# Softmax over rows of 1024: the first tile's load split into two 64-partition transfers on two queues, and one store moved from ACT's queue to Pool's

## The chip, the cores and the metric

The kernel runs on one core of a Trainium2 chip. The metric is the device time of one execution in microseconds (us); lower is better. Before the change the median of three runs is 317.25 us. The engines that matter here are VectorE (DVE), ScalarE (ACT) and GpSimd (Pool), and SyncE (SP), which only issues transfers. The 16 DMA engines of the core move all data between HBM, where the tensors live, and SBUF, the on-chip memory of 128 partitions in which the engines compute.

## The reference

`x` is 32 x 512 x 1024 float32, so 16384 rows of 1024 numbers, 67.11 MB; the output has the same size. The temperature is 0.5.

```python
scaled = x / temperature
shifted = scaled - np.max(scaled, axis=-1, keepdims=True)
exp_x = np.exp(shifted)
return (exp_x / np.sum(exp_x, axis=-1, keepdims=True)).astype(np.float32)
```

Each row is its own softmax. Every number is read once and written once, so 134.2 MB have to pass the DMA engines.

## The kernel before, in words

The rows are cut into 11 blocks, which the kernel calls passes. A pass is one tile `xt` of 128 partitions; passes 0 to 9 hold 12 rows in each partition (12 x 4 KB = 49152 B of consecutive memory, 6 MB in all), and pass 10 holds 8 rows (32768 B in each partition, 4 MB). Four tile buffers exist (`BUFS = 4`). A pass is worked on in place in two or three groups of 4 or 6 rows per partition (`PASSES`): pass 0 is 4, 4, 4; passes 1 to 9 are 6, 6; pass 10 is 4, 4.

For a group there are three steps. `maximum` (L69, L72) is one DVE reduction over the group's rows and one small DVE multiplication that makes the bias. `exponential` (L78) is one ACT activation per row, which also sums the row. `divide` (L90, then L93 or L96) is a small DVE reciprocal and either one DVE multiplication of the whole group (passes in `WHOLE`) or one per row.

Each engine runs its instructions in the order in which the program lists them, and the program writes that order out by hand: first four loads, then for each group g its maximum and exponential, and after them the divide of group g-1 and, when that was the last group of a pass, the store of that pass. In passes 9 and 10 the divide and the store come ahead of the next maximum (`ALONE`).

`load` (L60) issues one transfer for a whole pass from SP's queue; the profile calls that queue q1. The first four loads wait for nothing. Load 4 and the later ones are issued from inside `store`, one with each pass, and SP waits there until the store of the pass that last used the buffer has landed. `store` (L108) issues one transfer for a whole pass: from Pool's queue (q0, whose descriptors are made by software) for passes 0 to 5, which is what `BY_POOL = 6` says, and from ACT's queue (q10) for passes 6 to 10. On ACT the store stands behind the exponentials of the following group, on Pool behind nothing but the stores before it. Ahead of store 0 Pool makes a tiny copy out of tile 2 (L106), so that store 0 isn't issued before tile 2 has landed.

In the trace the first DVE reduction and ACT's load of its exponential table both start when tile 0 has landed, at 18.25 and 18.30 us.

Of the kernel before, what the change touches and what calls it, by code (L numbers as in the profile page):

```python
# [1 line left out]

# [4 lines left out]

PASSES = [[4, 4, 4]] + [[6, 6]] * 9 + [[4, 4]]  # L10
BUFS = 4

WHOLE = (2, 3, 4, 6, 8)


BY_POOL = 6

ALONE = 9


@with_exitstack
def kernel(
    ctx: ExitStack,
    tc: tile.TileContext,
    x: bass.AP,
    temperature: bass.AP,
    out: bass.AP,
):
    nc = tc.nc
    f32 = mybir.dt.float32  # L30
    scale = 1.0 / float(temperature)
    extreme = mybir.AluOpType.max if scale > 0 else mybir.AluOpType.min

    P = 128
    xf = x.flatten_outer_dims()
    of = out.flatten_outer_dims()
    n, d = xf.shape
    rows = [sum(ks) for ks in PASSES]
    assert sum(rows) * P == n

    data = ctx.enter_context(tc.tile_pool(name="data", bufs=BUFS))
    stats = ctx.enter_context(tc.tile_pool(name="stats", bufs=4))


    groups = []
    for i, ks in enumerate(PASSES):
        for j, k in enumerate(ks):
            groups.append((i, sum(ks[:j]), k))

    def dram(t, i):  # L50
        block = t[P * sum(rows[:i]) : P * sum(rows[: i + 1]), :]
        return block.rearrange("(p k) d -> p k d", p=P, k=rows[i])

    tiles, small = [], []

    def load():
        i = len(tiles)
        if i < len(PASSES):
            xt = data.tile([P, rows[i], d], f32, name="xt")
            nc.sync.dma_start(out=xt, in_=dram(xf, i))  # L60
            tiles.append(xt)

    def maximum(g):
        i, a, k = groups[g]
        top, bias, sums, recip = (
            stats.tile([P, k], f32, name=name) for name in ("top", "bias", "sums", "recip")
        )
        small.append((bias, sums, recip))
        nc.vector.tensor_reduce(  # L69
            out=top, in_=tiles[i][:, a : a + k, :], axis=mybir.AxisListType.X, op=extreme  # L70
        )
        nc.vector.tensor_scalar_mul(bias, in0=top, scalar1=-scale)  # L72

    def exponential(g):
        i, a, k = groups[g]
        bias, sums, _ = small[g]
        for b in range(k):
            nc.scalar.activation(  # L78
                tiles[i][:, a + b, :],
                tiles[i][:, a + b, :],  # L80
                mybir.ActivationFunctionType.Exp,
                bias=bias[:, b : b + 1],
                scale=scale,
                accum_out=sums[:, b : b + 1],
            )

    def divide(g):
        i, a, k = groups[g]
        _, sums, recip = small[g]
        nc.vector.reciprocal(recip, sums)  # L90
        if i in WHOLE:
            xt = tiles[i][:, a : a + k, :]
            nc.vector.tensor_mul(xt, xt, recip.unsqueeze(2).to_broadcast([P, k, d]))  # L93
            return
        for b in range(k):
            nc.vector.tensor_scalar_mul(  # L96
                tiles[i][:, a + b, :], in0=tiles[i][:, a + b, :], scalar1=recip[:, b : b + 1]
            )

    def store(g):  # L100
        i, a, k = groups[g]
        if a + k == rows[i]:
            if i == 0:


                nc.gpsimd.tensor_copy(stats.tile([P, 1], f32, name="seen"), tiles[2][:, 0, 0:1])  # L106
            queue = nc.gpsimd if i < BY_POOL else nc.scalar
            queue.dma_start(out=dram(of, i), in_=tiles[i])  # L108
            load()

    with tc.manual_schedule():
        for _ in range(BUFS):
            load()
        for g in range(len(groups) + 1):

            alone = g < len(groups) and groups[g][0] >= ALONE and groups[g][1] == 0
            if g > 0 and alone:
                divide(g - 1)  # L120
                store(g - 1)
            if g < len(groups):
                maximum(g)
                exponential(g)
            if g > 0 and not alone:
                divide(g - 1)
                store(g - 1)


# [1 line left out]
_INS = ['x', 'temperature']  # L131
_OUTS = [((32, 512, 1024), 'float32')]

_NUMBERS = {'temperature': 0.5}


# [26 lines left out]
```

## Time and profile before

| what | us |
|---|---|
| median of three runs (lowest, highest) | 317.25 (317.19, 320.41) |
| span of the profiled execution, first to last instruction | 315.8 |
| DVE busy in that span | 256.9 |
| ACT busy | 148.3 |
| Pool busy | 3.7 |
| first tile: issued, landed for DVE | 0.74, 18.25 |
| first store issued on Pool | 47.89 |
| store of pass 6 issued on ACT | 211.22 |
| last store issued on ACT | 301.35 |

The profile is of one execution and gives its span, with no other time of its own; the median of the runs lies 1.45 us above that span. A row of the page with 40 digits or numbers cuts the span into 40 slices of 7.9 us; a digit is the busy share of a slice in tenths, and 9 is 90% or more. The DMA row is the mean over the 16 DMA engines, and GB/s is what they moved, booked at the packets' starts. A DMA packet in these records is one partition's row of a tile, 49152 B or 32768 B, moved by one of the 16 engines, or one of 4 B with which an engine reports that its part of a transfer is done. In a table of windows the columns are the window, its length, the busy time of DVE, ACT and Pool with the number of instructions, the clock of TensorE (not used here), the DMA share and GB/s. In a timeline a line gives start, duration, engine, source line and operation; in brackets is the idle time ahead of it and what ended it.

### The profile page before, as it was taken

How to read it: one execution, taken by the hardware profiler on the slowest of the kernel's cores; microseconds unless marked ns; L12 is line 12 of the kernel's file. 1: busy time of each engine (PE TensorE's matmuls, PEld its weight loads, DVE VectorE, ACT ScalarE, POOL GpSimd, SP SyncE). 2: the span in 40 equal slices, each digit the busy share in tenths (PEclk: the TensorE clock that was granted, in tenths of full speed). 3: DMA queues.
4: the chain of work that ended last, by engine and by line, in shares of the span. 5: the costliest groups of instructions: out<-in, count | busy, mean ns of one | idle time of the engine just before them, and what ended most of it. 6: DMA issues, size and time to landing. Idle time of an engine off the chain costs nothing.

```text
span 315.8 us, 525 instructions
## 1 busy us (share of the span) xinstructions
DVE 256.9 (81%) x147; ACT 148.3 (47%) x257; POOL 3.7 (1%) x11
## 2 busy tenths in 40 slices
DVE  0069999999999899979976994999199999969710
ACT  0029636775461807344471744074416802953700
POOL 0000001000000000000000000000000000000000
DMA  8999999999999999999999999999999999999996
GB/s 305 473 417 423 461 411 399 399 468 430 400 479 417 417 461 411 430 467 405 442 448 399 455 442 405 467 424 417 461 417 430 455 401 463 411 452 411 455 411 270
DMA packets 3171, 134.24 MB, mean 425 GB/s; under 512 B 352, under 2 KB 352, under 8 KB 352
## 3 DMA queue, kind: packets, MB, share of 16 engines
q1 hardware_dynamic: 1584, 67.11, 49.7%
q0 software_dynamic: 864, 37.75, 27.6%
q10 hardware_dynamic: 720, 29.36, 21.5%
q14 instruction: 3, 0.02, 0.0%
HBM read 67.11 MB, written 67.11 MB: 425 GB/s over the span
## 4 chain that ended last, share of the span: by engine, by line
DMA 47%; DVE 28%; ACT 11%; issue 9%; DVEq 0%; SPq 0%; POOLq 0%
DMA xt<-in_x_dram 25%; DMA out_dram<-xt 22%; DVE top L69 16%; ACT xt L78 11%; DVE xt L96 8%; DVE xt L93 2%; DVE bias L72 0%; DVE recip L90 0%; DVEq L158 0%; SPq L60 0%; POOLq L108 0%
## 5 line engine op out<-in xcount | busy, mean ns | idle before, releaser
L78 ACT ACTIVATE xt<-xt,bias 128x1024 f32<-128x1024 f32 x128 | 145.2, 1135 | 131.7 <-DVE recip L90 70.6
L69 DVE TENSOR_REDUCE top<-xt 128x6 f32<-128x6144 f32 (+1 forms) x23 | 139.9, 6083 | 37.8 <-DMA xt<-in_x_dram 37.8
L93 DVE TENSOR_TENSOR xt<-xt,recip 128x6144 f32<-128x6144 f32 x10 | 65.6, 6558 | 0.4
L96 DVE TENSOR_SCALAR xt<-xt,recip 128x1024 f32<-128x1024 f32 x68 | 46.2, 749 | 0.5
L78 ACT ACTIVATION_READ_ACCUMULATOR xt<-xt,bias 128x1 f32 x128 | 23.9, 187 | 0.0
L78 ACT ACT_TABLE_LOAD x1 | 1.3, 1283 | 18.3 <-DMA xt<-in_x_dram 18.3
L90 DVE RECIPROCAL recip<-sums 128x6 f32<-128x6 f32 (+1 forms) x23 | 4.2, 182 | 5.0 <-ACT xt L78 5.0
L108 POOL DMA_DIRECT2D out_dram<-xt x6 | 3.3, 554 | 129.6 <-ACT xt L78 82.7
L72 DVE TENSOR_SCALAR bias<-top 128x6 f32<-128x6 f32 (+1 forms) x23 | 3.9, 171 | 0.8
L106 POOL COPY seen<-xt 128x1 f32<-128x1 f32 x1 | 0.2, 185 | 46.9 <-DMA xt<-in_x_dram 46.9
L144 POOL MEMSET const-uint8-127<- 128x1 uint8 x1 | 0.1, 103 | 0.0
L144 POOL MEMSET const-bfloat16-1.0<- 128x1 bf16 x1 | 0.1, 102 | 0.0
L144 POOL MEMSET const-float32-0.0<- 128x1 f32 x1 | 0.1, 99 | 0.2 <-issue 0.2
L144 POOL MEMSET const-float32-1.0<- 128x1 f32 x1 | 0.1, 98 | 0.0
## 6 DMA issues: line engine op xcount, KB each, us to landing
xt<-in_x_dram SPq DMA_DIRECT2D x10, 6144.0 KB, 36.4
out_dram<-xt POOLq DMA_DIRECT2D x6, 6144.0 KB, 35.9
out_dram<-xt ACTq DMA_DIRECT2D x4, 6144.0 KB, 31.9
xt<-in_x_dram SPq DMA_DIRECT2D x1, 4096.0 KB, 34.9
out_dram<-xt ACTq DMA_DIRECT2D x1, 4096.0 KB, 13.5
```

Of the source, the lines that this page charges most:

```text
L69: nc.vector.tensor_reduce(out=top, in_=tiles[i][:, a : a + k, :], axis=mybir.AxisListType.X, op=extreme)
L72: nc.vector.tensor_scalar_mul(bias, in0=top, scalar1=-scale)
L78: nc.scalar.activation(tiles[i][:, a + b, :], tiles[i][:, a + b, :], mybir.ActivationFunctionType.Exp, bias=bias[:, b : b + 1], scale=scal ...
L90: nc.vector.reciprocal(recip, sums)
L93: nc.vector.tensor_mul(xt, xt, recip.unsqueeze(2).to_broadcast([P, k, d]))
L96: nc.vector.tensor_scalar_mul(tiles[i][:, a + b, :], in0=tiles[i][:, a + b, :], scalar1=recip[:, b : b + 1])
L106: nc.gpsimd.tensor_copy(stats.tile([P, 1], f32, name="seen"), tiles[2][:, 0, 0:1])
L108: queue.dma_start(out=dram(of, i), in_=tiles[i])
L144: nc = _bacc.Bacc("TRN2", target_bir_lowering=False, num_devices=1)
```

## The change

The load of pass 0 is issued as two transfers of 64 partitions each: partitions 0 to 63 from SP's queue and partitions 64 to 127 from ACT's queue. Neither waits for anything. All other loads stay as they were. `BY_POOL` goes from 6 to 7, so the store of pass 6 is issued by Pool and no longer by ACT: Pool issues seven stores, ACT four.

```diff
-BY_POOL = 6
+BY_POOL = 7
...
             xt = data.tile([P, rows[i], d], f32, name="xt")
-            nc.sync.dma_start(out=xt, in_=dram(xf, i))
+            if i == 0:
+
+                half = P // 2
+                nc.sync.dma_start(out=xt[:half], in_=dram(xf, i)[:half])
+                nc.scalar.dma_start(out=xt[half:], in_=dram(xf, i)[half:])
+            else:
+                nc.sync.dma_start(out=xt, in_=dram(xf, i))
             tiles.append(xt)
```

## The prediction

> **What bounds the kernel now.** I read the page's slices first, then the queues, then a table of windows, then the DMA view of a few very short windows.
>
> ```profile
> DVE  0069999999999899979976994999199999969710
> ACT  0029636775461807344471744074416802953700
> DMA  8999999999999999999999999999999999999996
> q1 hardware_dynamic: 1584, 67.11, 49.7%
> q0 software_dynamic: 864, 37.75, 27.6%
> q10 hardware_dynamic: 720, 29.36, 21.5%
> ```
>
> The DMA row is full from the second slice to the last but one, while DVE, the busiest engine, starts in the third slice and has gaps to the end. The queues' shares add up to 98.8% of 16 engines' span. The queue sizes also tell how a load is cut: q1 has 1584 packets for 11 loads, 144 each, which is 128 rows and 16 reports: each of the 16 engines moves 8 partitions' rows and one report.
>
> ```profile
> 0.00:4.00 4.00, 0.00 (x0) 0.00 (x0) 0.21 (x4) 1.00 0.66 197
> 18.25:47.90 29.65, 29.23 (x24) 18.37 (x30) 0.19 (x2) 1.00 1.00 431
> 47.90:56.00 8.10, 8.03 (x6) 5.42 (x11) 0.66 (x1) 1.00 0.96 364
> 56.00:205.00 149.00, 135.16 (x63) 74.56 (x131) 2.66 (x5) 1.00 1.00 435
> 280.00:312.00 32.00, 19.08 (x21) 9.44 (x18) 0.00 (x0) 1.00 0.99 429
> ```
>
> Loads alone (18 to 48), loads with stores (56 to 205) and stores alone (280 to 312) all run at 429 to 435 GB/s and a DMA share of 0.99 or 1.00. So the end is set by the number of bytes at one fixed pace. Two places are short of it: the first microseconds, and 48 to 56, when Pool's first store joins.
>
> Next, four very short windows of the DMA view, each shorter than one packet: 1.7 to 2.5, 210 to 211, 211.85 to 212.95 and 217.3 to 218.5 us. The columns are packets, MB, share of 16 engines.
>
> ```profile
> q1 hardware_dynamic: 16, 0.79, 328.2%
> ...
> q0 software_dynamic: 15, 0.74, 171.2%
> ...
> q1 hardware_dynamic: 15, 0.74, 154.7%
> ...
> q10 hardware_dynamic: 15, 0.74, 141.9%
> ```
>
> A packet is booked where it starts, so a share gives its length: 1.547 x 16 x 1.1 us / 15 = 1.815 us for 49152 B, or 27.08 GB/s for an engine and 433 GB/s for 16. The others give 1.83 and 1.82 us on q0 and q10; the first 16 packets of the run lasted longer, 3.282 x 16 x 0.8 / 16 = 2.63 us. And the reader is to see that the engines take turns between queues in step: within 1 us, 15 of 16 start a packet of q0 and none one of q1, and a packet later it is the other way round.
>
> An engine has ten tiles x 8 rows x 2 directions = 160 packets of 1.815 us and 16 of 1.213 us (32768 B at that pace): 309.8 us. Add 1.76 us until the first packet starts, 0.81 us by which the first is longer (2.63 - 1.815), about 1.0 us in 48 to 56 ((433 - 364) x 8.1 / 433 = 1.3, part of it an artefact of booking at starts), and 1.3 us from the last packet's end at 314.5 to 315.8: 314.7 to 315.0 of 315.8 us. The median of the runs is 1.45 us above the span. I add costs to the span and carry that 1.45 along.
>
> **The change part by part.** *Store 6 from ACT to Pool.*
>
> ```profile
> 204.58 6.56 DVE L93 TENSOR_TENSOR xt<-xt,recip 128x6144 f32<-128x6144 f32 x1
> 211.22 0.97 ACTq L108 DMA_DIRECT2D out_dram<-xt  x1
> ```
>
> The divide of pass 6 ends at 211.14. ACT issues at 211.22, and the transfer's first packet starts at 217.33, since q0 still moves store 5 (its last row ends at 217.22). Pool waits for that same divide, its issue costs 0.53 us (median of its six), and its slowest start on an empty queue, store 0, is 4.4 us (47.89 to 52.26): ready at 215.5, before q0 is free. So q0 goes on at about 217.3 as q10 did. ACT loses a 0.97 us issue that lay before a wait of 6.4 us for the next bias at 217.84: nothing. If the cover were gone, store 6 would miss one turn, 1.8 us, while loads fill the engines, and load 10, which SP holds for store 6 until 246.68, would be that much later in a full queue. Pool has nothing behind store 6. I take 0, between 0 and 0.5.
>
> *The issue of the halves.* SP still issues four transfers by 2.8 us. ACT gets one more, 0.97 us as its first one cost, with 18.3 us of idle time around it:
>
> ```profile
> 0.74 2.05 SPq L60 DMA_DIRECT2D xt<-in_x_dram  x4
> 18.25 4.42 DVE L69 TENSOR_REDUCE top<-xt 128x4 f32<-128x4096 f32 x1 [18.25 <-DMA xt<-in_x_dram]
> 18.30 1.28 ACT L78 ACT_TABLE_LOAD   x1 [18.30 <-DMA xt<-in_x_dram]
> 22.91 1.15 ACT L78 ACTIVATE xt<-xt,bias 128x1024 f32<-128x1024 f32 x1 [3.33 <-DVE bias L72]
> ```
>
> Behind ACT's issue stand the table load and the first exponential, which waits for DVE until 22.91: cost 0. DVE's first maximum now needs two reports; a wait released by one shows 0.02 us of issue in the chain, so 0.02 more.
>
> *The halves themselves.* This decides. No transfer of 64 partitions is in this trace. The lower end: the limit of 27.08 GB/s belongs to each DMA engine, and all 16 share each half, four rows apiece. Then each still moves 8 packets of tile 0, and the tile lands as before; the longer first packet may hide behind the other queue's (-0.8 us), or be paid twice, or the second queue's joining costs what 48 to 56 cost (+1.0). The upper end: the limit belongs to the part of SBUF that an engine reaches. In a 128-partition transfer each engine has eight partitions of its own. In a half, 16 engines have 64 partitions between them, so two must share what one had, and since they take turns in step they are on the same half together. Each packet then lasts up to 2 x 1.815 = 3.63 us, eight in a row 29.0 instead of 14.5: +14.5 us, with no work to fill it, since the half that isn't being written waits in every engine's other queue.
>
> Which one? The pace is the same for reading HBM, writing it and both, and on three queues, so neither HBM nor the queue sets it; engine and SBUF side remain, and the trace doesn't separate them. A third arrangement is that a half goes to only eight engines: the same eight for both halves give 16 packets in a row for them, again +14.5 us, because each engine's total sets the end. A fourth, eight engines of its own for each half, is priced among the rivals. Of the four one costs nothing, and it needs both that all 16 engines serve each half and that the limit is the engine's own. I take the shared limit. The engines aren't quite in step: the 15 starts from 210 to 211 spread over 0.9 us, so two sharers overlap a little less than fully. With 0.2 us apart, each packet costs 1.815 - 0.2 = 1.6 us more, 8 x 1.6 = 13 us.
>
> [...]
>
> *What follows a late tile.* DVE starts 13 us later. From 18.25 to store 0 at 47.89 DVE is the chain (29.2 of 29.65 us busy), so store 0 goes to about 61; the loads of tiles 1 to 3 are 13 us later too, so the engines stay full and the rest of the run is moved as it stands. Sum: 315.8 + 13 + 0.02 + 0 = 328.8 span, 317.25 + 13 = 330 time.
>
> **The rivals.** *It makes no difference* (not slower). Place: the first 18 us; it decides if a 49152 B packet of a half still takes 1.815 us. For it speaks that this figure never moves between queues and directions. Tile 0 then lands near 18, at most some 4 us later if ACT's queue joins two turns late, and nothing follows from that, as loads alone keep the engines full until 2.6 + 32 x 1.815 = 60.7 us, and store 0's first packet moves only from 52.3 to 56. Time 317.25 - 0.8 to + 1.0: 316.4 to 318.3.
>
> *Each half goes to its own eight engines.* Then half two meets tile 1's rows in its engines and alternates: 16 packets, landing near 2.6 + 29 = 31.6 instead of 17.9. No engine time is wasted at first, but DVE starts 13.7 us later and store 0's first packet comes at 66, after the loads ran dry at 60.7: 5 us of idle DMA, and perhaps 2 to 4 more until store 1 follows. +5 to +9, 322 to 326. For it: nothing in the trace; against: a full transfer puts 8 rows on each engine evenly.
>
> *Faster by over 1%.* All that isn't bytes at the pace is 1.76 + 0.81 + 1.3 at the start and the join, 3.9 us, and the 1.76 stays; 3.2 us can't come out of the rest.
>
> **How the numbers follow.** Shared limit, or the same eight engines: 0.50, 326 to 332, point 330. Own eight engines: 0.08, 322 to 326. No difference: 0.40, 316.4 to 318.3. Faster by over 1%: 0.02. A measurement of this kernel can tell about 1%, 3.2 us. Slower is 0.50 + 0.08 = 0.58, same 0.40. Since neither main case may be left out, the range is 316.3 to 332; the likeliest case alone is 326 to 332.
>
> **What would show it.** Right: DVE's first reduction starts at 29 to 32 us, the DMA view of the first 18 us shows q1 and q10 packets of over 3 us and about half of 433 GB/s, and all later marks (store 0, last store) are 11 to 14 us later. Wrong: first reduction near 18 and packets of 1.8 us. Eight engines show as eight packets of a queue starting together instead of 16. Store 6 on q0 should start near the end of store 5 with no gap in the DMA share; a gap there would price the second part of the change.

## The result, and the profile after

The changed kernel takes 331.68 us (median of 6 runs, 331.43 to 332.03), the one before 317.22 beside it. The ratio is 1.0448 with a 95% interval of 1.0418 to 1.0477: 13.3 to 15.1 us slower. The profiled execution took 331.43 us and its span is 329.7, 13.9 us more than the 315.8 of before.

The page's slices and queues first, as for the kernel before. A slice is now 8.2 us.

```profile
DVE  0000799999999999999995899499589998969710
DMA  8997999999999999999999999999999999999996
GB/s 191 203 268 197 406 453 423 435 447 412 460 401 459 400 471 400 459 406 453 435 423 453 412 459 400 465 406 454 417 441 435 429 453 404 461 425 423 441 427 278
q1 hardware_dynamic: 1520, 63.96, 47.3%
q0 software_dynamic: 1008, 44.04, 30.9%
q10 hardware_dynamic: 656, 26.21, 20.7%
```

The DMA row alone would mislead: it is full from the start. The GB/s row shows what happened: four slices at 191 to 268, and from the fifth on the old pace. The engines are busy with packets that take twice as long (3.65 us against 1.815, worked out below). The table of windows says the same with DVE's part in it.

```profile
4.00:18.25 14.25, 0.00 (x0) 0.00 (x0) 0.00 (x0) 1.00 1.04 221
18.25:31.00 12.75, 0.00 (x0) 0.00 (x0) 0.00 (x0) 1.00 0.87 185
31.00:62.00 31.00, 26.41 (x20) 15.54 (x26) 0.00 (x0) 1.00 1.02 431
70.00:219.00 149.00, 138.32 (x68) 76.46 (x133) 2.66 (x5) 1.00 1.00 434
```

Until 31 us the engines are 87 to 104% busy at 185 to 221 GB/s; after that at 431 to 434 as before. Two windows of the DMA view, 9.1 to 10.5 and 12.7 to 14.1 us, show what kind of packets these are (packets, MB, share of 16 engines):

```profile
q10 hardware_dynamic: 16, 0.79, 260.4%
...
q1 hardware_dynamic: 16, 0.79, 260.7%
```

All 16 engines start a packet of the ACT half within 1.4 us, and a turn later all 16 one of the SP half. A packet lasts 2.604 x 16 x 1.4 / 16 = 3.65 us; before it was 1.815. The timeline shows the issues and the first work on the tile, Pool's stores of pass 0 and of pass 6, and ACT's last store:

```profile
0.74 0.54 SPq L63 DMA_DIRECT2D xt<-in_x_dram  x1
0.75 0.56 ACTq L64 DMA_DIRECT2D xt<-in_x_dram  x1
...
35.18 4.42 DVE L75 TENSOR_REDUCE top<-xt 128x4 f32<-128x4096 f32 x1 [35.18 <-DMA xt<-in_x_dram]
...
64.68 0.67 POOL L114 DMA_DIRECT2D out_dram<-xt  x1 [1.59 <-DVE xt L102]
225.31 0.53 POOL L114 DMA_DIRECT2D out_dram<-xt  x1 [31.19 <-issue]
314.79 0.34 ACTq L114 DMA_DIRECT2D out_dram<-xt  x1
```

The two halves are issued within 0.01 us of each other; DVE starts 16.9 us later than before.

### The profile page after: what moved, and what is told of

Its sections match the earlier page's. It is cut to its first block, busy times and chain, and to the rows that moved or that the text cites. A ratio compares the mean times of both kernels' runs of the same rounds, so it can differ in the third digit from the quotient of the medians.

```text
span 329.7 us, 532 instructions
## 1 busy us (share of the span) xinstructions
DVE 256.9 (78%) x147; ACT 148.3 (45%) x257; POOL 4.7 (1%) x12
## 4 chain that ended last, share of the span: by engine, by line
DMA 67%; DVE 19%; ACT 8%; issue 0%; DVEq 0%; SPq 0%
DMA xt<-in_x_dram 34%; DMA out_dram<-xt 33%; DVE top L75 12%; ACT xt L84 8%; DVE xt L102 7%; DVE bias L78 0%; DVE recip L96 0%; DVEq L164 0%; SPq L66 0%
```

## The experiments

Theory T: within a half of 64 partitions two DMA engines share what one has for itself in a transfer of 128, and since the engines take turns in step (16 packets to a turn, above), both are on the same half at the same time. Rivals: the second queue at the start costs the time; any transfer of fewer partitions is slow; the moved store has a part. Each ratio is to the kernel before, run on the same chip in the same series. It is worked out from the single runs and not from the medians: the kernel before had medians of 317.40 to 317.75 us in these series, and its runs in a series lay 2.4 to 3.7 us apart. Each profile is of one run. Diffs are against the kernel before; behind the first one, the test for tile 0 and the plain load are mostly left out.

**The two parts of the change, each alone.**

```diff
-            nc.sync.dma_start(out=xt, in_=dram(xf, i))
+            if i == 0:
+                nc.sync.dma_start(out=xt[:64], in_=dram(xf, i)[:64])
+                nc.scalar.dma_start(out=xt[64:], in_=dram(xf, i)[64:])
+            else:
+                nc.sync.dma_start(out=xt, in_=dram(xf, i))
```

> The load of tile 0 split into two halves of 64 partitions on SP's and ACT's queues; store 6 stays on ACT. Theory (two engines share one part of SBUF's side within a half, so a packet lasts twice 1.815 us): the whole loss is here, 331 to 332 us, the first 16 packets on q10 again at 3.6 us. Rival (moving store 6 to Pool has a part in the loss): below 330.

Measured: 333.77 us, ratio 1.0475 (1.0409 to 1.0541); the first 16 packets on q10 last 3.64 us on average. That is 1.8 us above the time expected, but not in the load: by the packet records the engines lose 17.7 us of the first 40, as in the changed kernel (17.8). They lose 3.7 us behind 290 us, where the changed kernel loses 2.1; why isn't known.

```diff
-BY_POOL = 6
+BY_POOL = 7
```

> Only the store of pass 6 is moved from ACT to Pool. Theory: no cost, 317.2 within 0.5 us. Rival (a part of the loss comes from the store): above 318.5 us, with a gap in the DMA share near 215 us.

Measured: 317.92 us, 0.2 above what was expected in a series in which the kernel before took 317.72; ratio 0.9985 (0.9956 to 1.0014), so between 1.4 us faster and 0.4 slower. The split alone loses as much as the whole change (the intervals of 1.0475 and 1.0448 overlap); the store costs nothing that can be told.

**Is it the second queue, or the half?** Both halves on one queue, and, the other way round, two queues with all partitions each.

```diff
+                nc.sync.dma_start(out=xt[:64], in_=dram(xf, i)[:64])
+                nc.sync.dma_start(out=xt[64:], in_=dram(xf, i)[64:])
```

> Both 64-partition halves of tile 0 are issued from SP's queue, one after the other; ACT issues no load. Theory (the half's partitions are what limits): every packet of tile 0 still lasts 3.6 us, eight in a row, 331 to 332 us; DVE starts earlier than the 35.2 us of the changed kernel, at 31 to 32, since no other queue's packets stand between the halves and their reports, and the total doesn't follow that start. Rival (two hardware queues fighting at the start cost the time): packets of 1.8 us and 317 to 318 us.

```diff
+                nc.sync.dma_start(out=xt[:, :6, :], in_=dram(xf, i)[:, :6, :])
+                nc.scalar.dma_start(out=xt[:, 6:, :], in_=dram(xf, i)[:, 6:, :])
```

> Tile 0 is loaded by two transfers of all 128 partitions at the same moment, rows 0 to 5 of each partition from SP's queue and rows 6 to 11 from ACT's. Theory: each engine again has eight partitions of its own, a packet of 24576 B lasts 0.91 us and the total is that of before, 316.5 to 318.5 us. Rival (two queues at the start cost the time): 331 us, packets of 1.8 us for 24576 B.

Both halves on SP: 332.88 us, 0.9 above what was expected, ratio 1.0463 (1.0402 to 1.0524). Its table of windows:

```profile
4.00:18.25 14.25, 0.00 (x0) 0.00 (x0) 0.00 (x0) 1.00 1.07 221
18.25:31.00 12.75, 0.00 (x0) 0.00 (x0) 0.00 (x0) 1.00 0.90 185
```

The same 221 and 185 GB/s with a single queue. The start at 31 to 32 was missed: the last row ends at 33.18, and DVE starts at 34.21, 1.0 us after that.

Halves by rows on two queues: 318.73 us, 0.2 above what was expected, ratio 1.0011 (0.9978 to 1.0044). Its DMA view from 6 to 8 us:

```profile
q1 hardware_dynamic: 19, 0.47, 54.3%
q10 hardware_dynamic: 16, 0.39, 45.6%
```

0.543 x 32 / 19 = 0.91 us for 24576 B on each queue (32 is 16 engines x 2 us), the full 27 GB/s. Two queues at the same moment cost nothing that can be told, at most 1.4 us; half of the partitions does (1.0463 on a single queue).

**Which partitions share?** Tile 0 in three transfers, partitions 32 to 95 from SP and the outer ones from ACT; then the same three on SP alone; then quarters.

```diff
+                nc.sync.dma_start(out=xt[32:96], in_=dram(xf, i)[32:96])
+                nc.scalar.dma_start(out=xt[:32], in_=dram(xf, i)[:32])
+                nc.scalar.dma_start(out=xt[96:], in_=dram(xf, i)[96:])
```

> Tile 0 is loaded by three transfers: partitions 32 to 95 from SP's queue, 0 to 31 and then 96 to 127 from ACT's. Theory (what two engines share is the place in SBUF of partitions 32 apart in the same half of 64): partitions 32 to 95 have no two such, so SP's packets last 1.8 us, while ACT's stay at 3.6 us; 4 x 1.8 + 4 x 3.6 = 21.8 us for the tile instead of 14.5, 324 to 325.5 us in all. Rival (any transfer over fewer than 128 partitions is slow, whichever they are): all packets 3.6 us, 331 to 334 us. [...]

Measured: 327.36 us, ratio 1.03 (1.0253 to 1.0347), 2 us more than expected. The first 16 of SP's packets last 2.45 us on average, ACT's first 16 3.64. A reading of the 2.45 us that no window shows: in this order the turns mix, and while some engines write rows of 32 to 95, others are still on an outer part. So it was run once more on one queue (the diff is against this kernel):

```diff
-                nc.scalar.dma_start(out=xt[:32], in_=dram(xf, i)[:32])
-                nc.scalar.dma_start(out=xt[96:], in_=dram(xf, i)[96:])
+                nc.sync.dma_start(out=xt[:32], in_=dram(xf, i)[:32])
+                nc.sync.dma_start(out=xt[96:], in_=dram(xf, i)[96:])
```

> As with the three transfers of partitions 32 to 95, 0 to 31 and 96 to 127 before, but all on SP's queue, in this order, so that no turn between queues mixes them. Theory (partitions 32 apart in one half of 64 share): the first four packets of each engine last 1.815 us but for the longer first one, the next four 3.6 us; tile 0 takes 21.8 us of packets instead of 14.5, +7.3 us, 324.5 to 326 us. Rival (any transfer over fewer than 128 partitions is slow): eight packets of 3.6 us, 332 us and more.

Measured: 325.61 us, ratio 1.0239 (1.0164 to 1.0314), as T priced it. The table of windows of this kernel:

```profile
4.00:10.00 6.00, 0.00 (x0) 0.00 (x0) 0.00 (x0) 1.00 0.95 401
10.00:17.00 7.00, 0.00 (x0) 0.00 (x0) 0.00 (x0) 1.00 1.05 225
17.00:24.00 7.00, 0.00 (x0) 0.00 (x0) 0.00 (x0) 1.00 1.03 218
```

And its DMA view from 6.5 to 7.9 us, in the first of these windows:

```profile
q1 hardware_dynamic: 14, 0.69, 113.5%
```

Of partitions 32 to 95 a packet takes 1.135 x 16 x 1.4 / 14 = 1.82 us, the steady pace (the 401 GB/s count packets where they start, in a short window), and directly behind them 32 partitions go twice at about 220 (225 and 218). So it isn't the number of partitions: 0 to 63 is slow (3.57 us a packet at the start of the changed kernel, 1.641 x 16 x 1.9 / 13 = 3.84 with both halves on SP, from 5.5 to 7.4 us) and 32 to 95 is not, though both read as many bytes of HBM in the same strides. That partitions 32 apart in one half share was assumed before the run, and the paces agree with it for whole blocks of 32: 0 to 31 go at 225 GB/s by themselves and, with both halves on SP, at 221 together with 32 to 63, while 32 to 63 and 64 to 95 together run at the steady pace. Which partitions of two blocks share no run here shows.

```diff
+                nc.sync.dma_start(out=xt[:32], in_=dram(xf, i)[:32])
+                nc.sync.dma_start(out=xt[32:64], in_=dram(xf, i)[32:64])
+                nc.sync.dma_start(out=xt[64:96], in_=dram(xf, i)[64:96])
+                nc.sync.dma_start(out=xt[96:], in_=dram(xf, i)[96:])
```

> Tile 0 goes as four transfers of 32 partitions from SP's queue. Theory (two engines share): packets of 3.6 us as with halves, since 32 partitions reach as many places as 64 do, 331 to 334 us. Rival (the pace falls with the number of partitions): packets of about 7.3 us and 29 us more than the halves, near 361 us.

Measured: 333.32 us, ratio 1.0487 (1.0433 to 1.0542); the first 16 packets of the four transfers average 3.67 to 3.83 us. A quarter is no slower than a half (3.65 in the changed kernel). That 32 partitions reach as many places as 64 do was assumed; the equal packets agree with it.

**Elsewhere in the run: a load in the middle, and a store.**

```diff
+            if i == 6:
+                nc.sync.dma_start(out=xt[:64], in_=dram(xf, i)[:64])
+                nc.sync.dma_start(out=xt[64:], in_=dram(xf, i)[64:])
```

> The load of tile 6, in the middle of the run, goes as two 64-partition halves from SP's queue, with stores on Pool's queue beside it. Theory: the engines keep in step between queues, so each of its packets lasts 3.6 us and the store's packets between them 1.8 us; +13 to +14.5 us, 330 to 333 us. Rival (it is a matter of the first microseconds, or stores in between take the pressure off): below 322 us.

Measured: 331.43 us, ratio 1.0402 (1.0346 to 1.0457). The DMA view from 144 to 158 us:

```profile
q1 hardware_dynamic: 51, 2.36, 65.8%
q0 software_dynamic: 41, 2.02, 35.7%
```

Of the 51 packets on q1 three are reports; 0.658 x 16 x 14 / 48 = 3.07 us for a row of the half, 1.95 for a row of the store between. A little below 3.65, and the loss near its full size (1.0402 against 1.0448): it isn't a matter of the first microseconds.

```diff
+            if i == len(PASSES) - 1:
+                nc.sync.dma_start(out=dram(of, i)[:64], in_=tiles[i][:64])
+                nc.scalar.dma_start(out=dram(of, i)[64:], in_=tiles[i][64:])
+            else:
+                queue.dma_start(out=dram(of, i), in_=tiles[i])
```

> Loads as in the kernel before; the store of the last tile is split into two halves of 64 partitions, on SP's and ACT's queues. Theory, if reading SBUF is limited as writing is: the last store's packets of 32768 B last 2.43 us instead of 1.21, eight of them 9.7 us more, 326 to 328 us. Rival (only writing into SBUF is limited so): 317 to 318.5 us.

Measured: 325.37 us over four runs from 321.76 to 327.1, and 324.25 without the longest, which the ratio leaves out: 1.0194 (1.0114 to 1.0274), 3.6 to 8.7 us slower. Reading SBUF is limited too (2.23 us for a packet of one half, below, against 1.213), but less was lost than expected, and the windows show why:

```profile
303.00:309.00 6.00, 0.00 (x0) 0.00 (x0) 0.00 (x0) 1.00 1.00 311
309.00:312.60 3.60, 0.00 (x0) 0.00 (x0) 0.00 (x0) 1.00 1.01 410
312.60:322.50 9.90, 0.00 (x0) 0.00 (x0) 0.00 (x0) 1.00 0.33 86
```

Between 309 and 312.6 the two halves ran at almost full pace, 410 GB/s. The DMA view of 309 to 312 and of 313 to 313.8 us tells the difference:

```profile
q10 hardware_dynamic: 19, 0.62, 52.3%
q1 hardware_dynamic: 17, 0.56, 43.7%
...
q10 hardware_dynamic: 9, 0.29, 157.0%
q1 hardware_dynamic: 5, 0.00, 0.4%
```

In the first window packets of both halves start side by side, 17 and 19, and q1's last 0.437 x 48 / 17 = 1.23 us (48 is 16 engines x 3 us), q10's 1.32, against 1.213 undisturbed. In the second only one half is left (q1's five are reports), and its packets last 1.57 x 16 x 0.8 / 9 = 2.23 us. In this kernel a half was slow when all engines still at work were on it. ACT's queue joined later here than SP's (its first packet of the tile starts at 305.95), and by 309 the engines had fallen out of step, as the 19 and 17 packets show. In the last window the share is 0.33: only some of the engines still have rows to move, and the last packet starts at 319.57.

**One microsecond that came back.** The kernel before loses 1.0 us when Pool's first store joins (engine time worked out from the packet records, each packet's bytes spread evenly over its time, against 433 GB/s); the changed kernel loses 0.01. Load packets just then, before (51.3 to 53 us) and after (67 to 69.5 us):

```profile
q1 hardware_dynamic: 11, 0.54, 118.0%
q0 software_dynamic: 5, 0.25, 33.4%
```

```profile
q0 software_dynamic: 14, 0.69, 63.7%
q1 hardware_dynamic: 5, 0.25, 22.7%
```

1.18 x 16 x 1.7 / 11 = 2.92 us for a load row before, 0.227 x 16 x 2.5 / 5 = 1.82 after. Three kernels asked what takes this loss away. The first loads six of tile 0's rows twice; the second loads 512 B of each of 64 partitions that nothing reads; the third splits only the last of tile 0's twelve rows.

```diff
+            if i == 0:
+                nc.sync.dma_start(out=xt[:, :6, :], in_=dram(xf, i)[:, :6, :])
             nc.sync.dma_start(out=xt, in_=dram(xf, i))
```

> All loads over 128 partitions as in the kernel before, but six of tile 0's twelve rows are loaded once more ahead of it, which moves everything behind by 7 to 10 us: 325 to 328 us. It asks about the 1.0 us that the DMA engines lose in the kernel before when Pool's first store joins (48 to 56 us), and that none of the kernels with a tile 0 split over partitions loses. If it hangs on when in the run that store comes, the loss is gone here (below 0.1 us); if on the part-partition transfers, it is there (about 1.0 us).

Measured: 330.58 us in a single run, beside 317.72; 12.9 us more, above what was expected. The extra rows are 7.3 us at the steady pace. SP issued tile 0's own load only at 11.03 us, after the extra rows, which go to the same buffer, had ended at 10.68: in the first 20 us the engines lost 5.8 us instead of 2.8, and behind 290 us 4.7 instead of 2.3. Pool's first store was issued at 58.60, and the engines lost 1.18 us there. The loss doesn't hang on the time: the changed kernel, with that store at 64.68, and the kernel with partitions 32 to 95 on SP and the rest on ACT, with it at 56.13, don't have it.

```diff
+                warm = stats.tile([P, 128], f32, name="warm")
+                nc.sync.dma_start(out=warm[:64], in_=dram(xf, 0)[:64, 0, :128])
```

> The kernel before, with one more transfer ahead of tile 0's load on SP's queue: 512 B of each of 64 partitions into a tile that nothing reads. If any part-partition transfer at the start takes away the 1.0 us that is lost when Pool's first store joins, the packets of 48 to 56 us stay at 1.8 us and the time is 316.5 to 317.2 us; if it needs the lateness or the size of the split tile, the loss stays at about 1.0 us and the time is 317.5 to 318.5 us.

```diff
+                nc.sync.dma_start(out=xt[:, :11, :], in_=dram(xf, i)[:, :11, :])
+                nc.sync.dma_start(out=xt[:64, 11:, :], in_=dram(xf, i)[:64, 11:, :])
+                nc.sync.dma_start(out=xt[64:, 11:, :], in_=dram(xf, i)[64:, 11:, :])
```

> Tile 0 goes as rows 0 to 10 of all 128 partitions, and then row 11 in two halves of 64 partitions, all on SP's queue. Theory: only the packets of row 11 (4096 B) last twice as long, eight of them 8 x 0.15 = 1.2 us more; with the 1.0 us at 48 to 56 gone the sum is +0.2, without that +1.2 us: 317.5 to 319.2 us, against the 14 us of splitting all rows.

The 512 B kernel: 319.58 us, above both times expected, ratio 1.0058 (1.0027 to 1.0088), and the loss is still there, 1.03 us; tile 0's first packet starts at 2.52 us instead of 1.76, and the rest of what it costs isn't accounted for. The one-row kernel: 319.04 us, ratio 1.0054 (1.0019 to 1.0089), and the loss is gone (0.00); the split row's 128 packets of 4096 B average 0.28 us, where the steady pace gives 0.15. So part-partition rows of the tile take it away and a small transfer doesn't; why stays open. None of these kernels is faster than the one before.

## Why the prediction was right, point by point

The range of 316.3 to 332 held two answers, no difference and slower, and 331.68 lies 0.3 us below its end. What was right is the likeliest case, 326 to 332, and its mechanism as far as the runs show it.

**The cause.** Right: a limit that goes with the partitions in SBUF, with 16 engines on each half and all in step. The trace after shows the 16 engines in step (16 packets to a turn) and 3.65 us for each packet, and the experiments leave none of the rivals: one queue with halves is as slow (1.0463), two queues with all partitions each are not (1.0011), and the 64 partitions 32 to 95 run at full pace (1.82 us a packet). That it is two engines that share stays a reading of the factor of 2.0 (3.65 against 1.815); the records don't show which engines share. The arrangements with eight engines fall with the 16 packets that start together. The prediction gave this case half of the chance, together with that of the same eight engines, because the trace before couldn't tell the limit's place; a kernel with a 64-partition transfer would have.

**Its size: the term of 13 us.** Too small, by 2. It took 1.6 us for each of eight packets, on the ground that two sharers would be 0.2 us apart. Nothing of these 0.2 us shows. The first packet lasts 3.57 us (2.63 before), the second 3.83, the next five about 3.65, the last 3.82: 0.94 + 2.02 + 5 x 1.84 + 2.0 = 14.2. The first packet starts 0.3 us later, and the first packets of tile 1 last 2.37 instead of 1.815, 0.55 more: together 15.0. By the packet records the engines lose 17.8 us up to 36 us, against 2.8 up to 18 us before: 15.0. From that goes the 1.0 us at Pool's first store, which the prediction carried along as unchanged: 14.0, and the span grew by 13.9. The span was forecast to grow by 13.0, so two errors, 2.0 too little and 1.0 too much, partly cancelled, by luck: 0.9 us are left. The rest of the way from 330 to 331.68 is that the median lies 1.98 us above the span now, 1.45 before.

**The tile's landing, and store 0.** Wrong: 29 to 32 us was said, DVE starts at 35.18. With it store 0 was wrong: it was to be issued at about 61 and 11 to 14 us later, and is issued at 64.68, 16.8 us later. The last store, at 314.79, is 13.4 us later, as was said. 14.6 us of DVE's delay are the rows themselves: the halves' last one ends at 32.47, tile 0's before at 17.88. The other 2.3 us the step left out, and they come from the turns. ACT's queue joined at the engines' third turn (first packet at 9.13 us, SP's at 2.06), so its rows are the last; by their end q1 has gone on to tile 1, and the halves' reports wait for a turn of their own: the ACT half's come at 33.8 to 34.7 us, behind a row of tile 1 each, and DVE starts 0.5 us after the last of them. The lateness beyond the forecast cost nothing at the end, as the prediction argued: loads kept the engines at 431 GB/s from 31 to 62, and when store 0's first packet came, at 68.41 instead of 52.26, they were still at it, with 0.01 us lost.

**Store 6 on Pool, and the issues.** Right, as far as can be told. Issued at 225.31, its first packet starts at 233.25, with store 5's last row ending at 232.92, and from 219 to 235 us the DMA share is 1.00 at 434 GB/s; alone it gave 0.9985 (0.9956 to 1.0014). ACT's extra issue took 0.56 us of 35 idle ones.

**The case against a faster kernel.** Its sum of 3.9 us leaves out the 1.3 us from the last packet's end to the end of the span, which the sum of the whole span has. Nothing else hung on it.

## What to carry to other kernels

In a kernel that keeps the DMA engines full, let each transfer cover all 128 partitions and split by rows if it must be split; here that cost nothing that could be told (1.0011, 0.9978 to 1.0044), and splitting at partition 64 cost about the tile's own transfer time once more (15.0 us; its eight packets take 14.5 at the steady pace). A busy DMA row isn't a fast one (a share of 1.04 went with 221 GB/s, 1.00 with 434): read GB/s and the length of a packet beside it. When a limit's owner decides a forecast and the trace can't name it, count the arrangements that are possible and price each.

## What the runs showed of the hardware that was not expected

- Partitions 32 to 95, alone on one queue, took 1.82 us a packet behind a longer first (1.688 x 16 x 1.6 / 16 = 2.70), 0 to 63 took 3.57 to 3.84: here it was decided by where the 64 partitions lie, not by their number.
- Halves of the last store were slow only while the engines were on the same one: 1.23 to 1.32 us for a packet of 32768 B with both halves mixed, 2.23 with one left. This stands on one kernel.
- When Pool's first store joins, 0.86 to 1.18 us are lost in the seven kernels that load all rows of tile 0 over 128 partitions (a load row lasted 2.92 us on average in the kernel before), and at most 0.01 in the seven that split rows of it by partitions (1.82 us in the changed kernel). Neither the time of the store nor a second queue explains it: with tile 0 split by rows over two queues the loss is there, with both 64-partition halves on one queue it isn't. Its cause stays open.
- A transfer of 512 B from 64 partitions, ahead of all others, cost 0.27 to 0.88% (0.9 to 2.8 us); 0.76 us of it is the later start of tile 0's first packet.
